# All splits of weights in the second block on VectorE, none on GpSimd

## The chip, the cores and the metric

The kernel runs on one core of a Trainium2 chip. The metric is the device time of one execution in microseconds, median of three runs. Engines are named as in the profile: PE (TensorE) multiplies matrices, PEld loads its weights, DVE is VectorE, ACT is ScalarE, POOL is GpSimd, SP is the engine whose queue issues most loads.

## The reference, cut to what matters

Two blocks one after the other on 512 tokens of width 1024, in fp32. The first block (a gated delta rule and a latent attention) is not touched. The second has two layers of this form:

```python
for i in range(2):
    g = norm_gains[i]
    f = swiglu(rmsnorm(h, g[0]), ffn_gate[i, 0], ffn_up[i, 0], ffn_down[i, 0])   # 1024 -> 2816 -> 1024
    h = h + 0.5 * rmsnorm(f, g[1])
    mix = hybrid_mixer(rmsnorm(h, g[2]), ..., w_in[i], ..., w_out[i])
    h = h + rmsnorm(mix, g[3])
    f = swiglu(rmsnorm(h, g[4]), ffn_gate[i, 1], ffn_up[i, 1], ffn_down[i, 1])
    h = h + 0.5 * rmsnorm(f, g[5])
    gate = sigmoid(rmsnorm(h, g[6]) @ w_ple_gate[i])
    h = h + rmsnorm((p[i] @ w_ple[i]) * gate, g[7])
```

`rmsnorm(x, g)` is x / sqrt(mean(x²) + eps) * g over the 1024 features. So behind each product stands a norm of its result, an addition to `h`, and a norm of `h` for the next product.

## The kernel before

**Products.** Tokens lie along the free axis in two `HALVES` of 256, features on the 128 partitions in 8 tiles. An fp32 product is made of three fp32r matmuls: each operand is split into a rounded high part H and a rest L, and H·H, H·L and L·H are added in PSUM (`fm`, `acc`). A weight tile comes by `w()` (L72 to 83): `raw` (L61 to 69) issues the load into a tile `wraw`, ACT copies it to fp32r as `wH` (L78), and `wL` = `wraw` − `wH` is one subtraction (L80) of 128x1024 elements, on DVE with `l="v"` (the default), on GpSimd with `l="g"`. This subtraction is what the text calls a split. In the second block, outside attention, there are three `wraw` tiles and eight pairs `wH`, `wL`, taken in turn.

**Where GpSimd splits.** In the second block: in `ffn`, the gate and up weights of the first four feature tiles of part 0 (`gw(ff, "gg")`, L1108), 8 splits in each of four FFNs; in the mixer, the `wvd` weights (L1307), 4 in each of two; in `ple`, the `wpg` weights (L1483), 8 in each of two. That is 56. Another 36 are in the first block.

**Norms between products.** `SumSq.add` (L149 to 160) squares each tile of a result on ACT (`ss_q`, L159) and adds it up on DVE (`ss`, L160). `sums` (L133) lets PE add over the partitions, `rsq` (L108 to 125) makes the reciprocal root on DVE in 12 or 13 instructions of 128x2 elements (`rq_v`, `rq_i`, `rq_j`, three Newton steps of `rq_a`, `rq_b`, `rq_y`, at times `rq_p`), `bcast` (L141) lets PE spread the result over the partitions. `norms` (L185) then makes `nt` (L191) and `h` (L193) and the squares of `h`; `prenorm` (L177) makes `ny` (L171), `xnH` (ACT, L101) and `xnL` (DVE, L105), the operand of the next product. All of this is a generator: `later` starts it, and `pull(n)` lets it take n steps between the products of the stage that follows (`down` L1097 and `gu` in an FFN, `f` L1491 in PLE).

**What sets the order.** The program is written in one order, and a scheduler of the tile library re-orders the instructions by priority and its own idea of how busy each engine is. Each engine then runs its instructions strictly in the order that results. So who does a split also decides where the instructions around it stand on every engine. Loads queue on SP in the same way.

Of the kernel before, what the change touches and what calls it, by code (L numbers as in the profile page):

```python
# [26 lines left out]
class Kern:  # L27
# [1027 lines left out]
    def ffn(self, l, j, g_out, g_next):  # L1055

        nc, I = self.nc, self.I
        X = (self.xnH, self.xnL)
        with ExitStack() as ctx:
            p = self.pool(ctx, "ffn", 1)  # L1060
            f = self.f
            NA = 4
            A = {}

            def gu(W, ff, c):
                if ff not in A:
                    A[ff] = tuple(p.tile([128, T], F32R, name="a" + z, bufs=9) for z in "HL")
                pg, pu = self.ps("g"), self.ps("x")
                n = c[1] - c[0]
                self.acc(pg[:, :n], self.fm(W[0], X, range(8), 0, c))  # L1070
                self.acc(pu[:, :n], self.fm(W[1], X, range(8), 0, c))
                s = p.tile([128, T], F32, name="fs", bufs=2)[:, :n]
                a = p.tile([128, T], F32, name="fa", bufs=2)[:, :n]
                nc.scalar.activation(s, pg[:, :n], AF.Silu)
                nc.vector.tensor_tensor(a, s, pu[:, :n], op=ALU.mult)  # L1075
                self.split(A[ff][0][:, c[0]:c[1]], A[ff][1][:, c[0]:c[1]], a, h="v")

            def gw(ff, l2="vv"):
                return [self.w(I["gu"][l, j, ff, z], 8, 128, l=l2[z]) for z in range(2)]

            ss = [self.SumSq(self) for _ in HALVES]

            def down(W, part, dm, c):
                k0, k1 = PARTS[part]
                n = c[1] - c[0]
                ps = self.ps("x" if dm % 2 else "g")
                prs = []
                for k in range(k0, k1):
                    aH, aL = A[k]
                    prs += [(W[0][:, k - k0], aH[:, c[0]:c[1]]), (W[0][:, k - k0], aL[:, c[0]:c[1]]),  # L1090
                            (W[1][:, k - k0], aH[:, c[0]:c[1]])]
                self.acc(ps[:, :n], prs)
                fk = f[:, dm, c[0]:c[1]]
                if part == 0:
                    nc.scalar.activation(fk, ps[:, :n], AF.Copy)
                else:
                    nc.vector.tensor_tensor(fk, fk, ps[:, :n], op=ALU.add)  # L1097
                if part == len(PARTS) - 1:
                    ss[0 if c[0] == 0 else 1].add(fk)

            def dw(part, dm):
                k0, k1 = PARTS[part]
                return self.w(I["dn%d" % part][l, j, dm], k1 - k0, 128)

            for part, (k0, k1) in enumerate(PARTS):
                ffs = list(range(k0, k1))
                if part == 0:
                    ws = {ff: gw(ff, "gg") for ff in ffs[:NA]}  # L1108
                    for c in HALVES:
                        for ff in ffs[:NA]:  # L1110
                            gu(ws[ff], ff, c)
                            self.pull(4)
                        self.pull()
                    ffs = ffs[NA:]
                for ff in ffs:
                    gu(gw(ff), ff, (0, T))
                if part < len(PARTS) - 1:
                    for dm in range(8):
                        down(dw(part, dm), part, dm, (0, T))
                else:  # L1120
                    ws = [dw(part, dm) for dm in range(8)]
                    for z, c in enumerate(HALVES):
                        for dm in range(8):
                            down(ws[dm], part, dm, c)
                            self.pull(2)
                        self.later(self.norms(ss[z], c, f, g_out, 0.5, g_next))
# [81 lines left out]
    def mixer(self, l, G):  # L1208

        nc, I = self.nc, self.I  # L1210
# [5 lines left out]
        with ExitStack() as ctx:  # L1216
# [5 lines left out]
            gg = p.tile([128, 8], F32, name="gg")  # L1222
# [75 lines left out]
            with ExitStack() as c2:  # L1298
# [5 lines left out]
                latH = p2.tile([128, 3, T], F32R, name="latH")  # L1304
                latL = p2.tile([128, 3, T], F32R, name="latL")
                ws = [self.w(I["win"][l, z], 8, 128) for z in range(3)] + [self.w(I["wkr"][l], 8, 64)]
                wv = [[self.w(I["wvd"][l, g, z], 4, 256, l="g") for z in range(2)] for g in range(2)]  # L1307
                kr = [p2.tile([32, T], F32, name="kr%d" % z) for z in range(2)]
                for c in HALVES:
                    n = c[1] - c[0]  # L1310
# [138 lines left out]
            ws = []  # L1449
# [20 lines left out]
    def ple(self, l, G, g_next):  # L1470

        nc, I = self.nc, self.I
        X = (self.xnH, self.xnL)
        with ExitStack() as ctx:
            p = self.pool(ctx, "ple", 1)
            f = self.f
            last = g_next is None
            ws, pe = [], []
            for c in HALVES:
                ss = self.SumSq(self)  # L1480
                for dm in range(8):
                    if c[0] == 0:
                        ws.append(self.w(I["wpg"][l, dm], 8, 128, l="g"))  # L1483
                        pe.append(p.tile([128, T], F32, name="pe", bufs=8))
                        nc.sync.dma_start(pe[dm], self.ple_dram[l, dm])
                    ps = self.ps("x" if dm % 2 else "g")[:, :256]
                    self.acc(ps, self.fm(ws[dm], X, range(8), 0, c))
                    t = p.tile([128, 256], F32, name="pt", bufs=2)
                    nc.scalar.activation(t, ps, AF.Tanh, scale=0.5)
                    fk = f[:, dm, c[0]:c[1]]  # L1490
                    nc.vector.scalar_tensor_tensor(fk, t, 1.0, pe[dm][:, c[0]:c[1]], op0=ALU.add, op1=ALU.mult)  # L1491
                    ss.add(fk, 0.5)
                    self.pull(2)
                self.later(self.norms(ss, c, f, G[7], 0.5, g_next, out=self.O["out"] if last else None))
# [254 lines left out]
```

## Time and profile before

| | |
|---|---|
| three runs | 3104.26, 3106.38, 3122.17 us |
| median | 3106.38 us |
| the profiled execution | 3119.48 us |
| its span | 3117.7 us |
| PE busy | 2818.9 us, 90% |
| DVE busy | 1728.3 us, 55% |
| ACT busy | 1082.3 us, 35% |
| POOL busy | 460.7 us, 15% |
| splits on DVE | 353, mean 1157 ns |
| splits on GpSimd | 92, mean 2471 ns |

The span is what the profiler saw of the program; the execution's own time has 1.8 us more around it. A busy PE is one with matmuls in flight.

### The profile page before, as it was taken

The numbers are of one execution on the slowest core, as the hardware profiler recorded it, in microseconds if no ns is written. First come the engines' busy times: TensorE is split into PE (matmuls) and PEld (weight loads), VectorE is DVE, ScalarE is ACT, GpSimd is POOL, SyncE is SP. The second block draws the span as 40 slices with busy tenths as digits, with TensorE's granted clock in tenths as the row PEclk, the third lists the DMA queues.
The fourth block names the chain that finished last, engine by engine and source line by source line (L and its number), as shares of the span: only waits on it lengthen the run. The fifth ranks groups of instructions, "written<-read, shape, count | busy, mean of one in ns | idle before, by whom it ended". The sixth has DMA issues, their size and how long they took to land.

```text
span 3117.7 us, 41758 instructions
## 1 busy us (share of the span) xinstructions
PE 2818.9 (90%) x15792; PEld 2376.6 (76%) x15792; DVE 1728.3 (55%) x3701; ACT 1082.3 (35%) x2078; POOL 460.7 (15%) x361
## 2 busy tenths in 40 slices
PE   6999699999999986978999988999987887999987
PEld 2878588678888885767888887888886666988877
DVE  6678907766333484668523378423375467623357
ACT  3443225433222232664322233322232474322223
POOL 3023211422000021422000022000011331000010
PEclk8999779999999987999999999999998789999998
DMA  5325341442323236843323221323234763232321
GB/s 193 104 97 173 92 127 44 144 147 90 106 90 101 66 120 185 215 151 112 107 94 98 88 89 55 115 91 98 88 107 132 216 195 117 89 97 92 97 73 55
DMA packets 138017, 354.51 MB, mean 114 GB/s; under 512 B 36912, under 2 KB 41392, under 8 KB 136792
## 3 DMA queue, kind: packets, MB, share of 16 engines
q1 hardware_dynamic: 125752, 316.18, 33.5%
q10 hardware_dynamic: 9216, 23.07, 2.2%
q0 software_dynamic: 2848, 12.59, 1.2%
q8 instruction: 124, 2.03, 0.3%
q14 instruction: 77, 0.63, 0.1%
HBM read 296.21 MB, written 55.57 MB: 113 GB/s over the span
## 4 chain that ended last, share of the span: by engine, by line
PE 70%; DVE 15%; issue 6%; DMA 4%; ACT 4%; POOL 2%; SPq 0%; ACTq 0%; DVEq 0%; POOLq 0%
PE psg L87 31%; PE psx L87 27%; PE psn L87 3%; DVE ss L160 2%; PE psx L1196 1%; DVE big L529 1%; DVE h L193 1%; PE psn L141 1%; DVE wL L80 1%; DMA wraw<-in_wo 1%; ACT wH L78 1%; DVE cy L403 1%; DVE rq_y L120 1%; PE psn L133 1%; PE psg L1040 1%
## 5 line engine op out<-in xcount | busy, mean ns | idle before, releaser
L78 ACT ACTIVATE wH<-wraw 128x1024 fp32r<-128x1024 f32 (+2 forms) x445 | 445.0, 1003 | 1165.6 <-PE psg L87 574.9
L80 DVE TENSOR_TENSOR wL<-wraw,wH 128x1024 fp32r<-128x1024 f32 (+3 forms) x353 | 407.9, 1157 | 456.3 <-ACT wH L78 456.0
L87 PE MATMUL psg<-xnH,wH 128*128 128x512 f32 (+3 forms) x1528 | 546.9, 360 | 24.0 <-ACT xnH L101 13.7
L87 PE MATMUL psg<-xnL,wH 128*128 128x512 f32 (+3 forms) x1528 | 545.8, 358 | 9.7 <-DVE xnL L105 9.7
L87 PE MATMUL psg<-xnH,wL 128*128 128x512 f32 (+3 forms) x1528 | 547.3, 359 | 3.5 <-POOL wL L80 2.8
L80 POOL TENSOR_TENSOR wL<-wraw,wH 128x1024 fp32r<-128x1024 f32 x92 | 226.9, 2471 | 1912.6 <-ACT wH L78 1164.9
L87 PE MATMUL psx<-xnH,wH 128*128 128x512 f32 (+1 forms) x1120 | 391.4, 350 | 2.0 <-ACT wH L78 2.0
L87 PE MATMUL psx<-xnH,wL 128*128 128x512 f32 (+1 forms) x1120 | 390.8, 349 | 1.0 <-DVE wL L80 1.0
L87 PE MATMUL psx<-xnL,wH 128*128 128x512 f32 (+1 forms) x1120 | 391.5, 350 | 0.0
L87 PEld LDWEIGHTS psg<-xnH,wH 128*128 128x128 f32 (+2 forms) x1528 | 295.3, 194 | 65.2 <-ACT xnH L101 15.8
L87 PEld LDWEIGHTS psg<-xnL,wH 128*128 128x128 f32 (+2 forms) x1528 | 295.8, 194 | 50.8 <-DVE xnL L105 13.3
L87 PEld LDWEIGHTS psg<-xnH,wL 128*128 128x128 f32 (+2 forms) x1528 | 296.4, 194 | 43.3 <-POOL wL L80 3.5
L87 PEld LDWEIGHTS psx<-xnH,wH 128*128 128x128 f32 x1120 | 217.2, 194 | 29.0 <-ACT wH L78 2.4
L87 PEld LDWEIGHTS psx<-xnH,wL 128*128 128x128 f32 x1120 | 216.8, 194 | 27.9 <-DVE wL L80 1.5
L87 PEld LDWEIGHTS psx<-xnL,wH 128*128 128x128 f32 x1120 | 217.1, 194 | 25.8
L1075 DVE TENSOR_TENSOR fa<-fs,psx 128x512 f32<-128x512 f32 (+1 forms) x104 | 62.9, 605 | 270.5 <-PE psx L87 270.5
L160 DVE TENSOR_TENSOR ss<-ss,ss_q 128x256 f32<-128x256 f32 x252 | 141.4, 579 | 35.4 <-ACT ss_q L159 34.5
L87 PE MATMUL psg<-aH,wH 128*128 128x512 f32 (+1 forms) x464 | 159.1, 343 | 0.0
L87 PE MATMUL psx<-aH,wH 128*128 128x512 f32 (+1 forms) x464 | 158.4, 341 | 0.0
L87 PE MATMUL psx<-aL,wH 128*128 128x512 f32 (+1 forms) x464 | 158.3, 341 | 0.0
L87 PE MATMUL psx<-aH,wL 128*128 128x512 f32 (+1 forms) x464 | 158.3, 341 | 0.0
L87 PE MATMUL psg<-aL,wH 128*128 128x512 f32 (+1 forms) x464 | 158.1, 341 | 0.0
(568 smaller groups left out, 4841.2 us busy)
## 6 DMA issues: line engine op xcount, KB each, us to landing
wraw<-in_gu SPq DMA_DIRECT2D x176, 512.0 KB, 3.5
wraw<-in_dn SPq DMA_DIRECT2D x64, 448.0 KB, 3.2
wraw<-in_dn SPq DMA_DIRECT2D x32, 512.0 KB, 3.8
wraw<-in_wmod SPq DMA_DIRECT2D x24, 512.0 KB, 5.8
wraw<-in_wrest ACTq DMA_DIRECT2D x24, 512.0 KB, 3.6
wraw<-in_wo SPq DMA_DIRECT2D x24, 512.0 KB, 3.5
wraw<-in_win SPq DMA_DIRECT2D x22, 512.0 KB, 5.4
kh<-KD SPq DMA_DIRECT2D x32, 256.0 KB, 5.3
```

The source lines that it names most:

```text
L78: nc.scalar.activation(H[:, :n], raw[:, :n], AF.Copy)
L80: e.tensor_tensor(L[:, :n], raw[:, :n], H[:, :n].bitcast(F32), op=ALU.subtract)
L87: self.nc.tensor.matmul(ps, lhsT=l, rhs=r, start=start and i == 0, stop=stop and i == m - 1)
L120: nc.vector.scalar_tensor_tensor(z, b, 1.5, y, op0=ALU.add, op1=ALU.mult)
L133: self.nc.tensor.matmul(ps[:, 2 * c:2 * c + 2], lhsT=a[:, 128 * c:128 * c + 128], rhs=self.ones2[:a.shape[0]], start=i == 0, stop=i == len ...
L141: self.nc.tensor.matmul(ps[:, 128 * c:128 * c + 128], lhsT=rs[:, c:c + 1].to_broadcast([128, 128]), rhs=self.ident, start=True, stop=True)
L160: nc.vector.tensor_tensor(self.a[i], self.a[i], q, op=ALU.add)
L193: nc.vector.tensor_tensor(hk, hk, t, op=ALU.add)
L403: nc.vector.scalar_tensor_tensor(y, cb[:, o + j:o + j + n], cw[:, j:j + 1], y, op0=ALU.mult, op1=ALU.add)
L529: nc.vector.tensor_tensor(tm, A[:112, i:i + 1, i + 1:].to_broadcast([112, n, n]), A[:112, i + 1:, i + 1:].rearrange("q j c -> q c j"), op= ...
L1040: nc.tensor.matmul(pv[:, 128 * i0:128 * (i0 + ni)], lhsT=V[:, j, v:v + 64], rhs=R[:, c0:c0 + 128 * ni], start=j == 0 and y == 0, stop=b == ...
L1075: nc.vector.tensor_tensor(a, s, pu[:, :n], op=ALU.mult)
```

## The change

The three places in the second block that asked for GpSimd no longer do so, and the parameter that let `gw` ask for it is gone.

```diff
@@ ffn
-            def gw(ff, l2="vv"):
-                return [self.w(I["gu"][l, j, ff, z], 8, 128, l=l2[z]) for z in range(2)]
+            def gw(ff):
+                return [self.w(I["gu"][l, j, ff, z], 8, 128) for z in range(2)]
@@ ffn, part 0
-                    ws = {ff: gw(ff, "gg") for ff in ffs[:NA]}
+                    ws = {ff: gw(ff) for ff in ffs[:NA]}
@@ mixer
-                wv = [[self.w(I["wvd"][l, g, z], 4, 256, l="g") for z in range(2)] for g in range(2)]
+                wv = [[self.w(I["wvd"][l, g, z], 4, 256) for z in range(2)] for g in range(2)]
@@ ple
-                        ws.append(self.w(I["wpg"][l, dm], 8, 128, l="g"))
+                        ws.append(self.w(I["wpg"][l, dm], 8, 128))
```

The order of the instructions changes with it. On GpSimd, between the first layer's mixer and the second's (`S` belongs to attention, `hd` and `VD` are copies of `h` and of attention's values in HBM), 28 splits stood together:

```order
 L1173 TENSOR_TENSOR S_12279<-S_12279,rd 128x384
 L1173 TENSOR_TENSOR S_12285<-S_12285,rd 128x512
-L80 TENSOR_TENSOR wL<-wraw,wH 128x1024 x28
 L1228 DMA hd_20182<-h 128x4096
 L1206 DMA VD_20124<-vo_20524 128x4x128
```

They are gone, as are 12 ahead of the first mixer and 16 behind the second; nothing else moved on this engine.

On DVE, where the first layer's second FFN ends and PLE begins (stage D of the prediction), the reciprocal root for the first half's `xnH` stood like this before (`ss_15949` are the sums of the second half):

```order
 L112 TENSOR_SCALAR rq_v<-psn 128x2
 L160 TENSOR_TENSOR ss_15949<-ss_15949,ss_q 128x256
 L113 TENSOR_SCALAR rq_i<-rq_v 128x2
 L114 TENSOR_SCALAR rq_j<-rq_i 128x2
 L1097 TENSOR_TENSOR f<-f,psg 128x256
 L118 TENSOR_TENSOR rq_a<-rq_v,rq_j 128x2
 L119 SCALAR_TENSOR_TENSOR rq_b<-rq_a,rq_j 128x2
 L120 SCALAR_TENSOR_TENSOR rq_y_16113<-rq_b,rq_j 128x2
```

After the change the same stretch reads:

```order
 L112 TENSOR_SCALAR rq_v<-psn 128x2
 L160 TENSOR_TENSOR ss_15949<-ss_15949,ss_q 128x256
 L113 TENSOR_SCALAR rq_i<-rq_v 128x2
 L80 TENSOR_TENSOR wL<-wraw,wH 128x1024
 L114 TENSOR_SCALAR rq_j<-rq_i 128x2
 L1097 TENSOR_TENSOR f<-f,psg 128x256
 L118 TENSOR_TENSOR rq_a<-rq_v,rq_j 128x2
 L80 TENSOR_TENSOR wL<-wraw,wH 128x1024
 L119 SCALAR_TENSOR_TENSOR rq_b<-rq_a,rq_j 128x2
 L160 TENSOR_TENSOR ss_15949<-ss_15949,ss_q 128x256
 L120 SCALAR_TENSOR_TENSOR rq_y_16113<-rq_b,rq_j 128x2
```

Two splits have come into the first Newton step; three more stand in the two steps behind it, two in the second half's root, and one ahead of the sums.

On DVE, where the first layer's first FFN ends and the mixer begins (stage B), the second half's reciprocal root after the change:

```order
 L114 TENSOR_SCALAR rq_j<-rq_i 128x2
 L80 TENSOR_TENSOR wL<-wraw,wH 128x1024
 L118 TENSOR_TENSOR rq_a<-rq_v,rq_j 128x2
 L119 SCALAR_TENSOR_TENSOR rq_b<-rq_a,rq_j 128x2
 L80 TENSOR_TENSOR wL<-wraw,wH 128x1024
 L120 SCALAR_TENSOR_TENSOR rq_y_9539<-rq_b,rq_j 128x2
 L118 TENSOR_TENSOR rq_a<-rq_v,rq_y_9539 128x2
 L119 SCALAR_TENSOR_TENSOR rq_b<-rq_a,rq_y_9539 128x2
 L80 TENSOR_TENSOR wL<-wraw,wH 128x1024
 L120 SCALAR_TENSOR_TENSOR rq_y_9545<-rq_b,rq_y_9539 128x2
```

Three splits now stand inside this root. On SP the loads and their number stay; at stage D those of the next FFN, two of which stood among PLE's, now stand behind all of PLE's.

## Rows read from the trace of the kernel before

**Rows 1.** The page, parts 1 and 4: PE, and the chain that ended last.

```profile
PE 2818.9 (90%) x15792; PEld 2376.6 (76%) x15792; DVE 1728.3 (55%) x3701; ACT 1082.3 (35%) x2078; POOL 460.7 (15%) x361
...
PE 70%; DVE 15%; issue 6%; DMA 4%; ACT 4%; POOL 2%; SPq 0%; ACTq 0%; DVEq 0%; POOLq 0%
```

**Rows 2.** Windows D, E: length; PE PEld DVE ACT POOL busy; clock, DMA, GB/s.

```profile
1815.00:1850.00 35.00, 21.60 (x160) 20.65 (x158) 31.15 (x57) 13.90 (x26) 19.29 (x8) 0.85 0.39 123
1885.00:1930.00 45.00, 31.37 (x211) 30.45 (x210) 38.39 (x80) 19.00 (x41) 19.80 (x8) 0.85 0.31 94
```

**Rows 3.** Timeline of PE in D: start, length, ..., idle before it.

```profile
1839.57 0.98 PE L133 MATMUL psn<-ones,ss 128*128 128x2 f32 x4 [8.10 <-DVE ss L160]
...
1846.57 0.68 PE L141 MATMUL psn<-ident,rq_y 128*128 128x128 f32 x4 [1.25 <-DVE rq_y L120]
```

**Rows 4.** Timeline of POOL in stage D: the first three of eight splits.

```profile
1815.54 2.35 POOL L80 TENSOR_TENSOR wL<-wraw,wH 128x1024 fp32r<-128x1024 f32 x1 [352.25 <-DVE rq_a L118]
1821.00 4.95 POOL L80 TENSOR_TENSOR wL<-wraw,wH 128x1024 fp32r<-128x1024 f32 x2 [3.11 <-ACT wH L78]
```

**Rows 5.** Timeline of DVE in stage D.

```profile
1815.66 2.25 DVE L120 SCALAR_TENSOR_TENSOR rq_y<-rq_b,rq_y 128x2 f32<-128x2 f32 x1
...
1821.55 4.68 DVE L160 TENSOR_TENSOR ss<-ss,ss_q 128x256 f32<-128x256 f32 x2
...
1827.55 1.08 DVE L160 TENSOR_TENSOR ss<-ss,ss_q 128x256 f32<-128x256 f32 x3
...
1829.61 1.88 DVE L193 TENSOR_TENSOR h<-h,nt 128x256 f32<-128x256 f32 x1
...
1833.88 2.11 DVE L160 TENSOR_TENSOR ss<-ss,ss_q 128x256 f32<-128x256 f32 x1
1835.90 2.56 DVE L193 TENSOR_TENSOR h<-h,nt 128x256 f32<-128x256 f32 x1
...
1843.00 0.16 DVE L118 TENSOR_TENSOR rq_a<-rq_v,rq_y 128x2 f32<-128x2 f32 x1
1843.19 2.24 DVE L119 SCALAR_TENSOR_TENSOR rq_b<-rq_a,rq_y 128x2 f32<-128x2 f32 x1
...
1848.47 2.34 DVE L105 TENSOR_TENSOR xnL<-ny,xnH 128x256 fp32r<-128x256 f32 x3
```

**Rows 6.** Timeline of DVE in stage E: first and last of seven long rows.

```profile
1886.15 2.42 DVE L1491 SCALAR_TENSOR_TENSOR f<-pt,pe 128x256 f32<-128x256 f32 x1 [0.22 <-ACT pt L1489]
...
1919.34 3.05 DVE L105 TENSOR_TENSOR xnL<-ny,xnH 128x256 fp32r<-128x256 f32 x3 [0.66 <-ACT xnH L101]
```

**Rows 7.** Timeline of DVE in stage C: two splits, two of eight long rows.

```profile
1421.46 1.22 DVE L80 TENSOR_TENSOR wL<-wraw,wH 128x1024 fp32r<-128x1024 f32 x1
1422.59 0.42 DVE L160 TENSOR_TENSOR ss<-ss,ss_q 128x256 f32<-128x256 f32 x1
...
1425.47 1.25 DVE L160 TENSOR_TENSOR ss<-ss,ss_q 128x256 f32<-128x256 f32 x1 [0.54 <-ACT ss_q L159]
...
1461.21 2.35 DVE L105 TENSOR_TENSOR xnL<-ny,xnH 128x256 fp32r<-128x256 f32 x1
```

**Rows 8.** Timeline in stage A: DVE, then PE.

```profile
727.55 2.39 DVE L118 TENSOR_TENSOR rq_a<-rq_v,rq_y 128x2 f32<-128x2 f32 x1
...
735.28 1.19 PE L141 MATMUL psn<-ident,rq_y 128*128 128x128 f32 x4 [4.04 <-DVE rq_y L120]
```

**Rows 9.** Stage B: timeline of DVE, of ACT, then loads of line 68.

```profile
1111.72 3.10 DVE L105 TENSOR_TENSOR xnL<-ny,xnH 128x256 fp32r<-128x256 f32 x3 [2.14 <-ACT xnH L101]
...
1123.12 1.06 ACT L78 ACTIVATE wH<-wraw 128x1024 fp32r<-128x1024 f32 x1 [4.89 <-DMA wraw<-in_wvd]
...
DMA to landing us min/median/max: 11.7/11.7/11.7
```

**Rows 10.** Stage D: waits of SP's queue, then loads issued there.

```profile
SPq L68 <- POOL wL L80: 49.6, 7, 24.6
...
wraw<-in_wpg SPq DMA_DIRECT2D x5, 512.0 KB, 3.5
```

## What I predict, before the result is known

> **What bounds the kernel now.** I read the page's engine table first: TensorE (PE) is busy 90% of the span, VectorE (DVE) 55%, GpSimd (POOL) 15%; and then the chain that ended last, where PE holds 70% and DVE 15% [rows 1]. So the kernel is bound by PE, and what can be won or lost is the time in which PE waits, most of it for DVE. Next I read the windows of the stretches in which GpSimd makes the splits that are to move. There are eight such stretches: A (711 to 760 us, the head of the first FFN), B and B' (the mixers' wvd, from 1100 and 2294), C and C' (the heads of the FFNs behind the mixers, from 1405 and 2600), D and D' (PLE's wpg, from 1813 and 3013) and E (the head of the FFN behind the first PLE, from 1883). In D PE works 21.60 of 35.00 us and DVE 31.15; in E 31.37 of 45.00 and 38.39 [rows 2]. In these stretches, then, it is DVE that sets the pace, and PE waits 13.4 and 13.6 us. The timeline of PE in D says on what: 8.10 us on the accumulator `ss` before the column sums (L133), 1.25 on `rq_y` before the broadcast (L141) [rows 3].
>
> Then I laid the timelines of POOL and DVE in D side by side. A GpSimd split lasts 2.35 us, two in a row 4.95 [rows 4]. Just when one starts, one DVE instruction becomes that long: the first split starts at 1815.54, and `rq_y`, 2 elements a lane, starts at 1815.66 and takes 2.25, where the like instruction at 1843.00 takes 0.16; over the pair from 1821.00, two `ss` additions take 4.68, where three take 1.08 elsewhere [rows 4, 5]. So a GpSimd split is not free work beside DVE: it holds up one DVE instruction for nearly its whole length.
>
> **The change, part by part.** 56 of GpSimd's 92 splits move to DVE: 8 in each of four FFN heads (A, C, E, C'), 4 in each of two mixers (B, B'), 8 in each of two PLEs (D, D'). The numbers of loads, of `wH` copies and of matmuls stay.
>
> *Price of a split on DVE.* It takes 1.22 us, and the next instruction starts 1.13 behind its start [rows 7]; I take 1.15. The 56 cost DVE 64.4 us. I leave the durations of `wH` and of the matmuls as they are.
>
> DVE works 31.15 of 35.00 us in D already, and gets more [rows 2]. The Trainium skill, page Perfetto Trace Analysis, section "Optimizing Scalar/DVE Operations", speaks against that: from a saturated DVE work should go over to GpSimd, not back, though the section itself doubts that it helps, since the two share a port. By its first half the sum would be +64, by the rows it is what follows; the rows decide, since they show the instructions that were held up, and the rule has a rival below.
>
> *What is taken away*, stage by stage, with 0.16 for a 128x2 and 0.36 for a 128x256 instruction that nothing holds up [rows 5]:
>
> D. The long rows are `rq_y` 2.25, two `ss` 4.68, `h` 1.88, `ss` 2.11, `h` 2.56, `rq_b` 2.24 and three `xnL` 2.34 [rows 5]. Less their normal times: 2.09 + 3.96 + 1.52 + 1.75 + 2.20 + 2.08 + 1.26 = 14.9. Eight splits on DVE: 9.2. Net −5.7. But the four terms from 3.96 to 2.20 (9.4) stand ahead of the sums, and PE cannot win more than the 8.10 it waits there [rows 3]; 1.3 of the gain finds PE at work. −4.4, twice (D').
>
> In the order after the change only one of the eight splits stands ahead of the sums; five stand between the sums and the end of the reciprocal-root chain, two in the second half's. So PE's wait before the sums nearly goes, and the wait before the broadcast takes over: 1.25 now, plus 5 x 1.15 less the 2.08, about 5. That is in the sum already, as the 9.2.
>
> E. Seven long rows of 11 instructions, from 1886.15 to 1919.34, last 18.9 us in all [rows 6]; one 128x2 and ten of 128x256 would take about 3.8. Stretch 15.1 less 9.2: −5.9. DVE is busy for 38.39 of 45.00 us here and PE waits 13.6 [rows 2], so I cap nothing.
>
> C. Eight long rows of 11 instructions, from 1425.47 to 1461.21, last 17.6 in all [rows 7]; less 3.8, less 9.2: −4.6, twice.
>
> A. Three Newton steps in a row, 2.39 (the first of them) + 2.28 + 2.26, end before the broadcast, where PE waits 4.04 [rows 8]. Unstretched they take 0.5, and two of the new splits stand among them: 6.9 − 0.5 − 2.3 = 4.1, capped at the wait: −4.0. The other six splits lie ahead of that, where nothing PE waits for is queued behind them; without that cover they would cost 6 x 1.15 = 6.9.
>
> B. Three `xnL` take 3.10 rather than 1.08 [rows 9]: at most −2.0, at least 0, if PE has products left. Between the two I take −1.2, twice. The splits that are left wait for their data anyway: the load took 11.7 us there, and ACT's `wH` waited 4.89 for it [rows 9]. In the new order those splits stand in a reciprocal-root chain, and in-order DVE waits in front of them. The 4.3 that the other two GpSimd splits stretch there is what I let this wait use up: 0.
>
> *Loads.* A raw tile is freed by its split. SP's queue waited 49.6 us for GpSimd's splits around D [rows 10], so freeing earlier or later shifts loads. In D the order on SP also changes: the first loads of the next FFN move behind all of PLE's. A load takes 3.5 us there [rows 10]. I cost this at nothing, since the splits of the next product have the 21.60 us of PE work in the stage as cover [rows 2]; the price without the cover is the first rival.
>
> Sum: D 2 x −4.4, E −5.9, C 2 x −4.6, A −4.0, B 2 x −1.2: −30.3 us. The profiled execution took 3119.48, 13 more than the median of the three runs, 3106.38; 3119.48 − 30.3 = 3089.2, and at the median (the gain scaled by 0.996) **3076.2**.
>
> **The rivals.**
>
> *The gain is given back by the ring of raw tiles.* On GpSimd, a split ran whenever its data had come. On DVE it runs where the order has put it, and the new order bunches it behind the sums. With three raw tiles the fourth load starts only when the first split has run: load 3.5, `wH` 1.06 [rows 9, 10], split 1.15: one turn is 5.7 us, at worst all of it on DVE's in-order path, in five stages (C, D, E, C', D'): 28.5 back of 30.3. From 3076 to 3105, middle 3095. For it: 49.6 us of waiting in the queue already [rows 10]. Against: ahead of the sums three tiles can be loaded and rounded before their turn comes.
>
> *Slower: the loads come late as in B.* If the loads in those five stages take 11.7 rather than 3.5 [rows 9, 10], the turn above costs 8.2 more in each: 41 more, net +11, so 3117. It decides from a load of 3.5 + 30.3/5 = 9.6 us if nothing of the first rival holds, earlier if some does, and passes 1% slower only from about 15.8. For it: the loads of the next FFN queue behind on the same SP queue. Against: DMA is busy 0.39 and 0.31 of the time in D and E [rows 2].
>
> *The splits are plain load on a full engine.* Were GpSimd's splits free for DVE, 56 x 1.15 = 64 us would come on top on the path: 3170. Against it stand the stretched rows [rows 5 to 8]; for it, that DVE sets the pace there. This is the first half of the rule of the Trainium skill's page Perfetto Trace Analysis, cited above.
>
> *PE's clock gives more.* The granted clock is 0.85 in D and E [rows 2]. If shorter waits kept it at full speed, 0.15 of PE's work there comes back: 3.2 us in D, 4.7 in E. At 3.2 to 4.7 in six stages 19 to 28 more: 3048 to 3057. Against: the waits shrink, they don't vanish.
>
> **How the numbers follow.** The forecast, 3060 to 3092 (half to one and a half times the sum), 0.55; ring of raw tiles 0.20; late loads 0.09; plain load 0.05; clock 0.11. The range for 8 in 10 is **3052 to 3106**: it leaves out late loads, plain load, and half of the clock's case, 0.19. A measurement of this kernel tells about 1% from no change, 31 us: below 3075.3 is faster, above 3137.4 slower. Faster: half of the forecast (0.29) and the clock, 0.40. Slower: plain load and the tail of late loads, 0.07. Within 1%: 0.53.
>
> **What would show each step.** After: POOL busy down by 56 x 2.4 = 136, to about 325; DVE busy near 1728 − 104 + 64 = 1690, though it does 56 more splits (104 is 56 times the mean stretch in D, 14.9/8). No 128x2 instruction on DVE near 2 us in these stages. PE's wait at L133 in D well below 8.10, at L141 well above 1.25. I am wrong if DVE stands idle in front of its own splits for more than about 2 us a stage (first rival; more than 6: second), or if the 128x2 rows stay long though GpSimd is quiet.

## The result, and the profile after

The changed kernel takes 3063.65 us (median of four runs, 3057.12 to 3073.96), the kernel before 3111.48 (four runs, 3104.26 to 3122.17). The ratio is 0.9847, 95% interval 0.9804 to 0.9889: faster by 1.5%, or 48 us. The forecast was 3076.2 us, a gain of 30 from the median of three runs (3106.38; a fourth has moved it to 3111.48), in a range from 3052 to 3106. The profiled execution of the changed kernel took 3062.55 us with a span of 3060.7.

The page after, parts 1 and 4 (answering [rows 1]):

```profile
PE 2795.3 (91%) x15792; PEld 2357.0 (77%) x15792; DVE 1687.9 (55%) x3757; ACT 1084.8 (35%) x2078; POOL 324.2 (11%) x305
...
PE 73%; DVE 11%; DMA 5%; issue 4%; ACT 4%; POOL 2%; SPq 0%; DVEq 0%; ACTq 0%; POOLq 0%
```

DVE is busy for 1687.9 us, with 56 splits more (409 instead of 353) and 40.4 us less than before; POOL for 324.2, 136.5 less. The chain that ended last lies on DVE for 11% instead of 15%.

Where the time went is seen best if the eight stages are cut at the same matmuls of line 87 in both traces, counted from the start. The windows of the stages, three rows of before and then three of after; columns: stretch, length, busy us of PE, PEld, DVE, ACT, POOL with their instructions, granted clock, DMA's share, GB/s. A and E stand for the eight; the sum is over all eight.

```profile
712.23:769.48 57.25, 50.13 (x369) 49.02 (x368) 43.70 (x81) 21.00 (x38) 19.24 (x8) 0.88 0.29 92
...
1882.79:1971.98 89.19, 75.11 (x574) 73.68 (x573) 72.47 (x175) 35.87 (x72) 19.80 (x8) 0.92 0.27 84
...
sum 637.94, PE 541.07 PEld 528.68 DVE 510.11 ACT 245.61 POOL 146.00; mean PE 67.63 PEld 66.08 DVE 63.76 ACT 30.70 POOL 18.25
...
701.30:751.53 50.23, 47.01 (x369) 46.16 (x367) 35.96 (x89) 21.68 (x38) 0.00 (x0) 0.93 0.33 105
...
1853.60:1931.71 78.11, 71.07 (x570) 69.91 (x569) 64.97 (x180) 36.32 (x72) 0.00 (x0) 0.96 0.31 96
...
sum 590.89, PE 527.95 PEld 517.96 DVE 465.93 ACT 247.18 POOL 8.34; mean PE 65.99 PEld 64.75 DVE 58.24 ACT 30.90 POOL 1.04
```

The eight stages took 637.94 us and now take 590.89: 47.1 less, about the whole difference of the medians. Of it 33.9 is idle time of PE (length less PE busy: 96.87 before, 62.94 after), and 13.1 is PE's own time for the same matmuls (541.07, 527.95). Most of that is the clock, which stands at one of two levels, 1.2 or 2.4 GHz. By the clock's records in the two traces PE worked in these stages for 78.3 us at the lower level before and for 57.6 after; at half the clock half of that difference is lost time, 10.3 us. Where the other 2.8 come from is open. The granted clock rose from 0.88 to 0.93 in A and from 0.92 to 0.96 in E; it did not rise in C, D and C' (0.94 to 0.93, 0.91 both times, 0.95 to 0.94). DVE is busy for 44.2 us less in these stages. Idle time of PE in each, worked out in the same way:

| stage | before | after | change | forecast |
|---|---|---|---|---|
| A | 7.12 | 3.22 | −3.9 | −4.0 |
| B | 12.24 | 11.29 | −1.0 | −1.2 |
| C | 10.60 | 6.09 | −4.5 | −4.6 |
| D | 15.11 | 9.27 | −5.8 | −4.4 |
| E | 14.08 | 7.04 | −7.0 | −5.9 |
| B' | 10.78 | 11.08 | +0.3 | −1.2 |
| C' | 11.87 | 6.02 | −5.9 | −4.6 |
| D' | 15.07 | 8.93 | −6.1 | −4.4 |

Outside the stages the two profiled executions differ too: up to stage A by 10.9 us (712.23 and 701.30). Nine kernels of the experiments have the same first block. In their profiles stage A starts between 690.2 and 712.6, in eight of them 6.8 to 22.1 us earlier than before and in one 0.4 later, so that this belongs to the execution and not to the change.

What PE waits for has changed as the order said it would (waits of PE over the whole span: us, times, longest; two rows of before, then the same two of after):

```profile
PE psn L133 <- DVE ss L160: 41.7, 12, 8.1
...
PE psn L141 <- DVE rq_y L120: 27.2, 21, 4.0
...
PE psn L141 <- DVE rq_y L120: 41.4, 18, 5.4
...
PE psn L133 <- DVE ss L160: 6.1, 7, 2.0
```

In stage D the timeline of DVE, then of PE, reads (answering [rows 3, 5]):

```profile
1805.69 1.22 DVE L80 TENSOR_TENSOR wL<-wraw,wH 128x1024 fp32r<-128x1024 f32 x1
...
1811.24 0.16 DVE L119 SCALAR_TENSOR_TENSOR rq_b<-rq_a,rq_y 128x2 f32<-128x2 f32 x1
1811.79 1.23 DVE L80 TENSOR_TENSOR wL<-wraw,wH 128x1024 fp32r<-128x1024 f32 x1 [0.40 <-ACT wH L78]
...
1815.61 1.23 DVE L80 TENSOR_TENSOR wL<-wraw,wH 128x1024 fp32r<-128x1024 f32 x1 [2.52 <-ACT wH L78]
1816.75 1.26 DVE L171 SCALAR_TENSOR_TENSOR ny<-h,gains,psn 128x256 f32<-128x256 f32 x3
...
1804.66 0.51 PE L133 MATMUL psn<-ones,ss 128*128 128x2 f32 x4
...
1813.24 1.19 PE L141 MATMUL psn<-ident,rq_y 128*128 128x128 f32 x4 [4.41 <-DVE rq_y L120]
...
1817.73 0.58 PE L87 MATMUL psg<-xnH,wH 128*128 128x256 f32 x1 [2.66 <-ACT xnH L101]
```

The 128x2 instructions last 0.16 us again. The sums (L133) start without a wait, where PE stood for 8.10 before. Instead PE waits 4.41 for the broadcast and 2.66 behind it. Five splits stand in that chain, and DVE stands idle in front of two of them for 0.40 and 2.52 us, until ACT has made their `wH`. That is the first rival's mechanism, at half its size.

In stage B' the same is worse (DVE, ACT, then PE; the last row is DVE in stage B):

```profile
2273.08 1.22 DVE L80 TENSOR_TENSOR wL<-wraw,wH 128x1024 fp32r<-128x1024 f32 x1 [6.49 <-ACT wH L78]
...
2272.00 1.06 ACT L78 ACTIVATE wH<-wraw 128x1024 fp32r<-128x1024 f32 x1 [7.35 <-DMA wraw<-in_wvd]
...
2276.93 1.12 PE L141 MATMUL psn<-ident,rq_p 128*128 128x128 f32 x4 [4.85 <-DVE rq_p L124]
...
1105.14 1.23 DVE L80 TENSOR_TENSOR wL<-wraw,wH 128x1024 fp32r<-128x1024 f32 x1 [4.83 <-ACT wH L78]
```

In front of a split of wvd DVE waits 6.49 us for `wH`, which ACT makes when the load has come, with the root's next step queued behind it, and PE waits 4.85 for that root. In B the like wait of DVE is 4.83. It is the wait for data that the prediction's term for B allowed 4.3 us for, and the second rival's mechanism in two stages that this rival did not name. It goes with B' having gained nothing.

### The profile page after: what moved, and what is told of

Read it like the earlier page. It is cut to its first block, busy times and chain, and to the rows that moved or that the text cites. A ratio compares the mean times of both kernels' runs of the same rounds, so it can differ in the third digit from the quotient of the medians.

```text
span 3060.7 us, 41691 instructions
## 1 busy us (share of the span) xinstructions
PE 2795.3 (91%) x15792; PEld 2357.0 (77%) x15792; DVE 1687.9 (55%) x3757; ACT 1084.8 (35%) x2078; POOL 324.2 (11%) x305
## 4 chain that ended last, share of the span: by engine, by line
PE 73%; DVE 11%; DMA 5%; issue 4%; ACT 4%; POOL 2%; SPq 0%; DVEq 0%; ACTq 0%; POOLq 0%
PE psg L87 33%; PE psx L87 29%; PE psn L87 3%; DVE wL L80 2%; PE psx L1196 1%; DVE big L529 1%; DMA wraw<-in_wvd 1%; PE psn L141 1%; DMA wraw<-in_wo 1%; DMA wraw<-in_win 1%; ACT wH L78 1%; DVE cy L403 1%; PE psg L1040 1%; PE psn L133 1%; ACT S L1168 1%
## 5 line engine op out<-in xcount | busy, mean ns | idle before, releaser
L80 DVE TENSOR_TENSOR wL<-wraw,wH 128x1024 fp32r<-128x1024 f32 (+3 forms) x409 | 476.0, 1166 | 475.3 <-ACT wH L78 474.5
L87 PE MATMUL psg<-aH,wL 128*128 128x512 f32 (+1 forms) x464 | 157.3, 339 | 0.0
```

The source lines that it names most:

```text
L80: e.tensor_tensor(L[:, :n], raw[:, :n], H[:, :n].bitcast(F32), op=ALU.subtract)
L87: self.nc.tensor.matmul(ps, lhsT=l, rhs=r, start=start and i == 0, stop=stop and i == m - 1)
```

## The experiments

Medians below are of each kernel's own runs; the kernel before was run beside them each time (3105.2 to 3108.9), and a ratio is against it. The changed kernel is at 3063.65; it was not run again beside the others, and the kernel before stood at 3111.48 beside it. So a distance to the changed kernel in us holds up to 6 us of drift; where that matters, the distance by the ratios stands with it (0.9847 for the changed kernel, 1% being 31 us).

**One part at a time.** Three kernels, in each of which one of the three edits stands and the other splits are GpSimd's, for instance with the FFN heads alone:

```diff
-                wv = [[self.w(I["wvd"][l, g, z], 4, 256) for z in range(2)] for g in range(2)]
+                wv = [[self.w(I["wvd"][l, g, z], 4, 256, l="g") for z in range(2)] for g in range(2)]
-                        ws.append(self.w(I["wpg"][l, dm], 8, 128))
+                        ws.append(self.w(I["wpg"][l, dm], 8, 128, l="g"))
```

> Only the 32 splits at the heads of the four FFNs move to VectorE; wvd and wpg stay with GpSimd. Theory (every GpSimd split holds up one VectorE instruction, each stage pays for itself): the gain is that of stages A, C, E and C', where between the profiles of before and after TensorE's idle time fell by 3.9, 4.5, 7.0 and 5.9, together 21.3 us, and the stages' lengths by 31.3; so 21 to 31 us under the kernel before, about 3083. Rival (the gain is one of the new order as a whole, or of the clock, and does not lie in the stages): anything under 10 us or over 40.

> Only the 16 splits of wpg (stages D and D') move to VectorE. Theory: TensorE's idle time fell by 5.8 and 6.2 us there, the stages' lengths by 5.0 and 8.7; so 12 to 14 us under the kernel before, about 3098. Rival (stage D gains only because the FFN head behind it is quicker too): under 5 us.

> Only the 8 splits of wvd (stages B and B') move to VectorE. Theory (these splits wait for late loads in front of VectorE, which eats what the missing hold-ups give): idle time of TensorE fell by 1.0 in B and rose by 0.3 in B', so within 2 us of the kernel before, no measurable difference. Rival (the whole 3.10 us row of xnL and the rest come back): 4 us or more faster, which this measurement would hardly tell, but the idle time in B and B' would.

Measured: FFN heads 3078.3 (ratio 0.9901, 0.9873 to 0.9929), wpg 3093.98 (0.9954, 0.9931 to 0.9978), wvd 3103.07 (0.9991, 0.9970 to 1.0011), the kernel before beside them 3108.88. That is 30.6, 14.9 and 5.8 us less, together 51 beside the 48 of all three at once. The parts add up, and each gains in its own stages: with the FFN heads alone PE's idle time fell by 3.9, 4.6, 6.1 and 5.8 us in A, C, E and C' and by 0.2 in D; with wpg alone by 5.8 and 6.1 in D and D'. In stages whose splits a kernel leaves alone, it moved by −1.7 to +1.5 us (D' −1.7 with the FFN heads alone). For wvd the interval holds no change, and PE's idle time in B and B' rose by 0.1 and 0.4. So the gain does not come from the new order as a whole. What the order within a stage gives beside the end of the hold-ups is not told apart by these three.

**Is it the hold-up?** Two kernels that keep the changed kernel's splits on DVE and make 48 of them (FFN heads and wpg) a second time, into a tile that nobody reads: once on GpSimd, once on DVE. A third lets GpSimd copy the raw tile instead. Shortened, the line that each of them adds for these 48:

```diff
+        D = self.wdp.tile([128, 1024], F32, name="wD", bufs=1)
+        nc.gpsimd.tensor_tensor(D[:, :n], raw[:, :n], H[:, :n].bitcast(F32), op=ALU.subtract)   # first
+        nc.vector.tensor_tensor(D[:, :n], raw[:, :n], H[:, :n].bitcast(F32), op=ALU.subtract)   # second
+        nc.gpsimd.tensor_copy(D[:, :n], raw[:, :n])                                             # third
```

> The changed kernel, in which GpSimd makes 48 splits (FFN heads and wpg, not wvd) a second time into a tile that nobody reads; VectorE still makes the ones that are used, in nearly the same order as in the changed kernel. Theory (GpSimd's 128x1024 subtraction holds up one VectorE instruction by about 1.9 us): 48 x 1.9 = 91 us come on VectorE on top of its own splits, and in stages where VectorE sets the pace most of it shows: about 3064 + 75 = 3140, between 3105 and 3150, with 128x2 rows of about 2 us back in the stages. Rival (the gain came from the new order, and GpSimd's work beside VectorE is harmless): within 10 us of 3064.

> The changed kernel, in which VectorE itself makes 48 splits (FFN heads and wpg) a second time into a tile that nobody reads; the counterpart of the run with GpSimd's second splits (3155.8, 92 us over the changed kernel). Theory (in these stages VectorE's time is the path's time; a split of its own costs 1.15 us of it, a split on GpSimd 1.9): 48 x 1.15 = 55 us more at most, 3104 to 3119. Rival (the second split hurts because it keeps the raw tile and wH longer, not by VectorE's time): as slow as with GpSimd's second splits, 3140 to 3160.

> The changed kernel, in which GpSimd copies the raw tile 48 times (128x1024, one input instead of two) where in the run with GpSimd's second splits it subtracted. Theory A (any GpSimd instruction on SBUF holds VectorE up for its length): 48 times the copy's length less 0.5 us over 3064, with one long VectorE row beside each; with a copy of 1.5 to 2.4 us 3110 to 3150. Theory B (only an instruction with two inputs holds it up): 3064 to 3075, and no long rows.

Measured: 3155.84 us with GpSimd's second splits (1.0155, 1.0122 to 1.0188), 92 over the changed kernel (96 by the ratios); 3103.24 with DVE's (0.9995, 0.9973 to 1.0018), 40 over (46); 3082.45 with GpSimd's copies (0.9928, 0.9906 to 0.9951), 19 over (25). A useless split on GpSimd, which no one waits for, thus costs more than twice as much as one on DVE. In the first kernel the rows of POOL, then of DVE, in stage C, then the window of stage E and the sum over the eight stages:

```profile
1423.88 2.34 POOL L80 TENSOR_TENSOR wD<-wraw,wH 128x1024 f32<-128x1024 f32 x1 [2.18 <-ACT wH L78]
...
1423.75 0.16 DVE L119 SCALAR_TENSOR_TENSOR rq_b<-rq_a,rq_y 128x2 f32<-128x2 f32 x1
1423.95 2.29 DVE L120 SCALAR_TENSOR_TENSOR rq_y<-rq_b,rq_y 128x2 f32<-128x2 f32 x1
...
1892.88:1993.75 100.87, 80.52 (x574) 78.86 (x573) 82.88 (x184) 36.17 (x73) 21.86 (x8) 0.85 0.24 74
...
sum 685.01, PE 556.76 PEld 544.08 DVE 557.25 ACT 245.69 POOL 140.47; mean PE 69.60 PEld 68.01 DVE 69.66 ACT 30.71 POOL 17.56
```

`rq_y` starts 0.07 us behind GpSimd's subtraction and lasts nearly as long, 2.29 against 0.16 for the row ahead of it. In all, 48 rows of DVE are held up like this, by 92.6 us together (each row's length less the median of like instructions). DVE's busy time in the stages is 557.25, 91.3 over the changed kernel's 465.93; the kernel is 92 us slower. That is over the forecast, 3140 and at most 3150. PE's idle time in the stages is up by 65.3 us (685.01 − 556.76 against 62.94), within the 75 that was expected, and its time for the same matmuls by 28.8. The latter is the clock: PE works for 114.6 us at the lower level in these stages, 57.0 more than in the changed kernel, and half of that is 28.5.

With the second splits on DVE, the sum over the stages:

```profile
sum 631.31, PE 534.82 PEld 524.31 DVE 515.08 ACT 247.13 POOL 8.27; mean PE 66.85 PEld 65.54 DVE 64.39 ACT 30.89 POOL 1.03
```

DVE has 49.2 us more, the stages take 40.4 more. So in these stages about four fifths of what is put on DVE comes out at the end, which is what "DVE sets the pace there" meant. The rival that the tiles are merely held longer expected 3140 to 3160 here, and that did not come. GpSimd's second split holds them longer than DVE's, though (2.47 against 1.22 us), so that this run alone does not settle it; the held-up rows do, since they come to 92.6 us of DVE's time, as much as DVE's busy time grew.

With the copies, POOL, then DVE, in stage C, and the sum:

```profile
1417.29 1.04 POOL L80 COPY wD<-wraw 128x1024 f32<-128x1024 f32 x1 [1.33 <-DMA wraw<-in_gu]
...
1417.20 0.17 DVE L113 TENSOR_SCALAR rq_i<-rq_v 128x2 int32<-128x2 int32 x1
1417.40 0.96 DVE L114 TENSOR_SCALAR rq_j<-rq_i 128x2 int32<-128x2 int32 x1
...
sum 607.87, PE 531.28 PEld 519.89 DVE 490.65 ACT 246.81 POOL 56.09; mean PE 66.41 PEld 64.99 DVE 61.33 ACT 30.85 POOL 7.01
```

A copy (one input) takes 1.04 us here, 1.08 in the median, and holds `rq_j` up for 0.8. Some 37 of the 48 copies hold a row of DVE up, by 26.1 us together. DVE's busy time is up by 24.7, the stages take 17.0 longer. So a GpSimd instruction with one input holds DVE up as well, only it is shorter; the theory that two inputs are needed falls. The expected 3110 to 3150 was worked out for a copy of 1.5 to 2.4 us; by its own rule, 48 x (1.08 − 0.5), it would have been 3092. The Trainium skill, page SBUF — State Buffer, section "SBUF: two separate sides", has GpSimd share a pair of ports with a VectorE instruction that has two inputs in SBUF or runs in a two-port mode; the one that starts first keeps the pair for its whole instruction. The 2.29 beside a 2.34 agrees with that (`rq_y` reads `rq_b` and `rq_y`). `rq_j`, 0.96 beside a 1.04, has one such input; whether it runs in a two-port mode no run here shows.

**Do the splits in the chain give gain back?** Here the splits from the third tile of wpg, and from the second feature tile of an FFN head, read a 1.0 made from the broadcast, so that they cannot stand ahead of it (shortened):

```diff
+        if c[0] == 0:
+            self.one = self.np_.tile([128, 24], F32, name="one", bufs=2)[:, :1]
+            self.nc.vector.tensor_scalar(self.one, rsB[:, :1], 0.0, 1.0, op0=ALU.mult, op1=ALU.add)
...
-        e.tensor_tensor(L[:, :n], raw[:, :n], H[:, :n].bitcast(F32), op=ALU.subtract)
+        e.scalar_tensor_tensor(L[:, :n], raw[:, :n], self.one, H[:, :n].bitcast(F32), op0=ALU.mult, op1=ALU.subtract)
```

> The changed kernel, in which the splits of FFN heads (from the second feature tile) and of wpg (from the third tile) read a 1.0 that VectorE makes from the first half's broadcast, so that they cannot stand ahead of it; as many splits as in the changed kernel, and 7 tiny instructions more. In the changed kernel five splits (5 x 1.14) and 2.9 us of waiting for wH stand between the sums and the first `ny` of stage D (11.5 us), while TensorE waits 4.4 before and 2.7 behind the broadcast. Theory (splits bunched in that chain give part of the gain back): these two waits fall below 3 us together, and 2 to 5 us come back in each of C, D, E, C', D': 3040 to 3054. Rival (the splits are needed right behind the broadcast anyway, and TensorE then waits for wL instead): within 5 us of 3064. Second rival (held splits hold their three raw tiles, loads start later): slower than 3070.

Measured: 3063.61 (0.9866, 0.9844 to 0.9888), the same as the changed kernel. DVE, then PE, around stage D, then PE in the changed kernel, and the sum over the stages with held splits:

```profile
1811.16 1.25 DVE L171 SCALAR_TENSOR_TENSOR ny<-h,gains,psn 128x256 f32<-128x256 f32 x3
...
1810.37 0.68 PE L141 MATMUL psn<-ident,rq_y 128*128 128x128 f32 x4 [0.70 <-DVE rq_y L120]
...
1843.34 1.19 PE L141 MATMUL psn<-ident,rq_y 128*128 128x128 f32 x4 [3.84 <-DVE rq_y L120]
...
1845.07 0.68 PE L141 MATMUL psn<-ident,rq_y 128*128 128x128 f32 x4 [0.77 <-DVE rq_y L120]
...
sum 590.97, PE 526.37 PEld 513.87 DVE 469.21 ACT 246.66 POOL 8.28; mean PE 65.80 PEld 64.23 DVE 58.65 ACT 30.83 POOL 1.03
```

The first `ny` stands at 1811.16 instead of 1816.75, and PE waits 0.70 for its broadcast instead of 4.41. But at 1843.34 it waits 3.84 for a later root, where it waits 0.77 in the changed kernel. No split stands ahead of that root, the last one ran at 1826.91; PE's products are through at 1838.5, before the sums, where the changed kernel still has 2.5 us of them behind the sums to fill the root's time. PE's idle time fell by 1.8 and 1.0 us in D and D', and rose by 0.4 to 1.2 in C, E and C'. The sum is 590.97 beside 590.89. The theory that 2 to 5 us a stage can be had by shifting these splits falls; PE came earlier and waited at the next root. That it is the amount of DVE's work between two products that counts, and not its place, agrees with this, but this is the only run that shifts splits.

**The ring of raw tiles.** A fourth raw tile needs room, so there is a kernel with two instead of three buffers for the norms' temporaries, and one that has the tile as well:

```diff
-        self.np_, self.nb = self.pool(ctx, "np2", 1), 3
+        self.np_, self.nb = self.pool(ctx, "np2", 1), 2
...
-        self.wadd(self.wx, 4, 0)
+        self.wadd(self.wx, 4, 1)
```

> The changed kernel with two instead of three buffers for the norms' temporaries in the second block (nt, ny, ss_q and the sums), only to make room for the next run's fourth raw tile; it is that run's comparison. Both theories: up to 15 us slower than 3064, if ACT and VectorE wait for each other's buffers.

> As the run before, with a fourth raw tile in the second block outside attention. Theory (the ring of raw tiles makes VectorE wait for its own splits, 2.9 us in stage D): that wait goes, 2 to 3 us in each of five stages, 10 to 15 us faster than the run before, and no VectorE row of line 80 with over 1 us of idle time on wH in D. Rival (the wait is ACT's order, or the loads themselves): within 3 us of the run before, and the wait in front of the fifth split of D stays above 2 us.

Measured: 3047.07 with fewer buffers alone (0.9817, 0.9794 to 0.9839), 3056.06 with the fourth tile (0.9842, 0.9813 to 0.9871). DVE in stage D of the former, then of the latter, and the sums over the stages of the latter and the former:

```profile
1807.12 1.23 DVE L80 TENSOR_TENSOR wL<-wraw,wH 128x1024 fp32r<-128x1024 f32 x1 [1.09 <-ACT wH L78]
...
1812.42 1.23 DVE L80 TENSOR_TENSOR wL<-wraw,wH 128x1024 fp32r<-128x1024 f32 x1 [0.78 <-ACT wH L78]
...
1815.10 0.87 DVE L171 SCALAR_TENSOR_TENSOR ny<-h,gains,psn 128x256 f32<-128x256 f32 x2 [1.38 <-PE psn L141]
...
sum 583.55, PE 525.48 PEld 515.38 DVE 464.91 ACT 249.93 POOL 9.35; mean PE 65.68 PEld 64.42 DVE 58.11 ACT 31.24 POOL 1.17
...
sum 582.21, PE 525.61 PEld 516.48 DVE 466.80 ACT 250.24 POOL 9.35; mean PE 65.70 PEld 64.56 DVE 58.35 ACT 31.28 POOL 1.17
```

The wait in front of a split is 0.78 with the fourth tile, but with fewer buffers alone it is 1.09 already, from 2.52 in the changed kernel; most of the fall is not the tile's. In C, D, E, C' and D' DVE stands idle in front of its splits for 20.6 us with the tile and 20.8 without it. So the tile hardly shortened these waits, and nothing came of it: the intervals overlap, the sums are 583.55 and 582.21. What the ring costs is thus not shown by this pair; a fourth tile does not win it back. With fewer buffers the kernel is 17 us faster by the medians, but 9 by the ratios (0.9817 and 0.9847, intervals that overlap) and 8.7 by the stages' sums. That was not expected; the order changes in many places, and the cause stays open.

**The first block's 36 splits, and two steps more.**

```diff
-                Ws, c = [w_[:, 0] for w_ in self.w(src, 1, 1024, l="g")], self.c4
+                Ws, c = [w_[:, 0] for w_ in self.w(src, 1, 1024)], self.c4
-                        W = self.w(I["wrest"][z], 8, 128, l="g", q=nc.scalar)
+                        W = self.w(I["wrest"][z], 8, 128, q=nc.scalar)
...
-            nc.gpsimd.tensor_tensor(u, u, v, op=op)       # rope_pair, in the last of the three
+            nc.vector.tensor_tensor(u, u, v, op=op)
```

> The changed kernel, and the 36 splits that GpSimd still makes in the first block move to VectorE too. Theory (worth of a move = what the split holds up on VectorE, less 1.15, and only where TensorE waits for VectorE): in the profile of the changed kernel these 36 stretch VectorE's instructions by 24.7 us in all, 0.7 each, since many run while VectorE has nothing to do or reads PSUM; 36 x 1.15 = 41 us come on; so no gain, 0 to 16 us slower, 3064 to 3080. Rival (VectorE is the better place for every split): 36 x 0.8, the mean gain of the 56, 25 to 30 us faster, about 3036.

> No split on GpSimd at all (also the first block's 36 on VectorE), and two buffers for the norms' temporaries in the second block. If the two gains add (3064 to 3042, and 3064 to 3047): about 3025. If both came from the order or the clock by luck: 3042 to 3047, or worse.

> As the run before, and the 26 additions of the rotary embedding (128x512, 1.30 us on GpSimd) on VectorE, where a like instruction takes 0.6. Theory (worth = what is held up less the cost on VectorE): they stretch VectorE by 11 us in all and would cost 26 x 0.6 = 16: 0 to 5 us slower than the run before. Rival (the shorter latency counts too; ACT waits 44.4 us for these results in the changed kernel): 5 to 15 us faster.

Measured: first block 3041.78 (0.9780, 0.9749 to 0.9811); with two buffers 3031.65 (0.9767, 0.9744 to 0.9791); with the rotary additions 3019.47 (0.9721, 0.9705 to 0.9737). The first of these is 22 us faster than the changed kernel (21 by the ratios), where I expected 0 to 16 slower: "what is held up, less 1.15" isn't the whole worth of a move in the first block. In the profiles stage A starts 18.9 us earlier (682.4 and 701.3), and all that follows takes as long (2359.2 and 2359.4); but kernels with one and the same first block lie up to 22 us apart there. A split's own length, 2.4 us on GpSimd, may count there too: the wait for a root at the kernel's start (2.30 at 37 us) is gone, and a long wait of PE got shorter and has another cause. PE in the changed kernel, then here:

```profile
361.81 1.46 PE L568 MATMUL psx<-Y,C 32*32 32x32 f32 x24 [23.04 <-DMA Y<-dX]
...
338.92 0.79 PE L87 MATMUL psg<-xnH,wL 128*128 128x512 f32 x1 [15.62 <-DVE wL L80]
```

How much of the 22 us is the shorter split, how much the end of the hold-ups and how much the new order was not taken apart. The two gains of 22 and 17 make 39, and 32 came; by the ratios it is 21 and 9, and 25 came. Whether they add is not told by that. The rotary additions, forecast at 0 to 5 us slower, made it 12 faster, as the rival had it: ACT's wait for their results fell from 45.1 to 14.8 us. How much of the 12 that is, and how much the end of their hold-ups, was not taken apart. The page's engine row of this last kernel, the fastest here, 2.8% under the kernel before:

```profile
PE 2783.9 (92%) x15792; PEld 2348.5 (78%) x15792; DVE 1698.4 (56%) x3819; ACT 1088.3 (36%) x2078; POOL 198.8 (7%) x243
```

## Why the prediction was right, and where it was too small

**What bounds the kernel, and the hold-up: right.** PE waits, DVE sets the pace in the eight stages, and a GpSimd split is paid for by DVE. The runs with second splits show both prices. One on GpSimd holds DVE up by 92.6/48 = 1.9 us, and the forecast had 14.9/8 = 1.9; that it also costs 92/48 = 1.9 us of the kernel is in part chance, since 28.8 of the 92 are PE's clock. One on DVE costs 40/48 = 0.8 us of the kernel (1.0 by the ratios), where the forecast had 1.15.

**The terms.** In idle time of PE the sum was good: −33.9 against −30.3. A, B and C came out within 0.2, which is closer than stages agree that nobody touched (up to 1.7 apart), so partly luck. D, D', E and C' gained 1.1 to 1.7 more. In D the cap looks like the wrong step: I let 1.3 us of the gain "find PE at work" because PE cannot win more than its 8.10 at the sums. But the sums came earlier in the new order, and the wait moved to the next place where PE stands, so that DVE's saving was not lost: 5.7 of uncapped net against 5.8 and 6.1 measured. No run tests the cap by itself. B' gained nothing, where its split waits for a late load.

**The step that failed is "I leave the durations of the matmuls as they are".** PE's time for them fell by 13.1 us, by the sum rows, 10.3 of it by the clock. That was one of the rivals, with 0.11 and 19 to 28 us; it came at about half its size, beside the forecast and not in its place. It is no accident of one execution: with the FFN heads alone A and E have a granted clock of 0.93 and 0.94 (before 0.88 and 0.92), and with GpSimd's second splits PE's time for the same matmuls is 28.8 us longer. The forecast of 30.2 plus these 13.1 plus the 3.6 by which the idle time was too small makes 46.9, beside 48 measured.

**The rivals.** The ring was there (2.9 us in D, half of the rival's 5.7); neither the held splits nor the fourth tile won anything back. The rival's middle of 3095 is not the middle of its 3076 to 3105, which is 3090. Late loads came in B and B' (4.83 and 6.49 us), not in the five stages of the rival. "Plain load" is refuted: 48 more splits on DVE do cost 40 us, but the 56 that moved took 99.7 us of hold-ups with them (over the trace of before, each held-up row's length less the median of like instructions; 104 was forecast).

**The signs.** DVE at 1690 and POOL at 325 were forecast, 1687.9 and 324.2 came (56 x 2.4 is 134, not 136; 136.5 came). No 128x2 instruction near 2 us is left in the stages. PE's wait at the sums fell and that at the broadcast rose, 1.25 to 4.41 in D, where I had said about 5. One sign misled: DVE's idle time in front of its own splits passed the 2 us a stage that should have meant the first rival (2.9 in D), and the 6 that should have meant the second (7.1 in B'). But before the change it was 2.0, 5.5 and 8.9 already in C, E and C'; over the eight stages it rose from 21.3 to 39.1, and the kernel got faster all the same.

## What to carry to other kernels

Lay the timelines of GpSimd and VectorE side by side before calling GpSimd's work free: a long row of a tiny VectorE instruction just behind the start of a GpSimd one is the price. A split is better where it costs VectorE least, own time against time held up, and where VectorE sets the pace the end result follows its busy time: four fifths of what was put on it came out at the end, and shifting splits within a stage changed nothing in the one run that did so. Where TensorE waits less, its clock may give something back too, here 10 us beside 34 of waiting.

## What was not expected of the hardware

- A GpSimd copy of 128x1024 fp32 takes 1.08 us (median of 48), its subtraction with two inputs 2.47, and both can hold VectorE up for nearly their length: 0.96 and 2.29 us on instructions that take 0.16. Every subtraction of the second block did so, and some 37 of the 48 copies.
- The granted clock was lower in stages where PE waits more: 0.84 to 0.85 in C, D and E with GpSimd's second splits, 0.91 to 0.96 in the changed kernel. Of the 94.1 us between these two in the eight stages, 28.5 are the clock's.
- PE's time in the eight stages, less half of what it worked at the lower clock level, is 498 to 502 us in the traces of all twelve kernels in which the eight stages were cut, while the time itself goes from 525 to 557. So nearly all of that difference is the clock.
- Fewer buffers for the norms' temporaries made the kernel 9 us faster by the ratios, within the noise, and 17 by the medians; no run here explains it.
